# Where a matmul's operands lie in on-chip memory: activation tiles, weight halves and raw weights placed first, on multiples of 512 bytes

## The chip, the core and the metric

The kernel runs on one core of a Trainium2 chip. The metric is device time in microseconds, from the launch's first instruction to its last with what lies around them; three runs of the kernel before gave 998.23, 998.87 and 999.73 us, median 998.87. Beside it stands one profiled execution, whose span (first to last instruction) is 996.9 us.

## The reference

A trunk of two layers on 256 positions of width 1024, in float32. Each layer normalizes its input, makes one wide projection, runs four mixers side by side, merges them under gates and adds a gated feed-forward:

```python
h = rms_norm(x, norm1_g)
z = h @ w_in
za, zb, zc, zd, zg = jnp.split(z, IN_SPLITS, axis=-1)
ya = retention(za, ret_gn_g)
yb = conformer_conv(zb, conv_w, conv_b, conv_ln_g, conv_ln_b)
yc = spatial_gating(zc, gmlp_ln_g, gmlp_ln_b, gmlp_ws, gmlp_bs)
yd = swa_attention(zd, swa_q_g, swa_k_g, swa_sinks, rel_bias)
ys = jnp.stack([ya, yb, yc, yd], axis=2).astype(w_branch.dtype)
branches = jnp.einsum('bsnc,ncd->bsnd', ys, w_branch)
gates = jax.nn.sigmoid(zg.reshape(B, S, N_BRANCH, D_MODEL))
mix = jnp.sum(gates * branches, axis=2)
x = x + (mix @ w_out).astype(x.dtype)
h = rms_norm(x, norm2_g)
gt, up = jnp.split(h @ w_ffn_in, 2, axis=-1)
return x + ((jax.nn.silu(gt) * up) @ w_ffn_out).astype(x.dtype)
```

## The kernel before, in words

The 256 positions are two tiles of 128 (t = 0, 1). All large products have the activations as the stationary operand and the weights as the moving one. Float32 precision is reached with three matmuls of type float32r: each operand is split into a high part, which is the value rounded to that type, and a low part, which is the rest.

```python
nc.tensor.matmul(ps, xh, hs, start=start, stop=False)
nc.tensor.matmul(ps, xh, ls, start=False, stop=False)
nc.tensor.matmul(ps, xl, hs, start=False, stop=stop)
```

These are lines 137, 138 and 139, the method mm; nearly all of TensorE's work goes through them. The moving tile is wh, wl, wh in turn, the stationary tile the high part twice and the low part once. A stationary block is 128 x 128, that is 512 bytes in each partition; a moving block has 512 columns (2048 bytes in each partition) or, in the narrow pieces, 256.

The stationary tiles are of two kinds. hT (act_tile, L184; one buffer for each t) holds the normalized activations, and the merged mix before w_out; it has 8 blocks for the high part and 8 for the low. yT (y_tile, L187; four buffers) holds a mixer's output before its branch product, and a piece of the feed-forward's inner activation before w_ffn_out; it has 4 and 4 blocks. The method cols (L141) runs hT over a unit of weights; chunk (L593), gates (L731), project (L773) and the first half of ffn (L788) call it. The method branch (L749) and out_mm inside ffn (L823) run yT, by mm itself. In gates and in branch, twelve matmuls (4 blocks x 3) go to one bank of PSUM before the next bank is taken.

Weights come from memory in units of 1 MB, each of two halves of 512 KB (fetch, L97): a load into raw (six buffers), then in part (L112) ScalarE casts it into wh (L114) and VectorE writes the difference into wl (L115); wh and wl have eight buffers each. take (L123) keeps the loads two units ahead of use. The opening (L232) writes the first half's cast and difference by hand (L252, L254), and warms TensorE up with bf16 matmuls on a small tile, warm, which is both operands (L265).

Beside this, four mixers run as tasks that are advanced at ticks between chunks: softmax attention (L311 to L418), convolution, whose 31 taps are VectorE instructions (L443), retention, and the spatial gating, whose products have ws as the stationary and gv as the moving tile (L585). Transposes go through TensorE with the data as the stationary tile and the identity as the moving one (L164, L814). The reciprocal roots are powers on GpSimd (L181), with the constant tile nhalf as the exponent.

Every SBUF tile comes from a pool. Pools lie one behind the other in the order in which they are made, and the tiles of one pool in the order of their first use, each start rounded up to 32 bytes. So a small tile made early (nhalf, 40 bytes; derived, 20; col, 600; rel, 32) shifts the remainder of all behind it.

Of the kernel before, what the change touches and what calls it, by code (L numbers as in the profile page):

```python
# [8 lines left out]
F32 = mybir.dt.float32  # L9
BF16 = mybir.dt.bfloat16  # L10
F32R = mybir.dt.float32r
# [5 lines left out]
P = 128  # L17
# [11 lines left out]
BRANCHES = (3, 0, 2, 1)  # L29
FF_CHUNKS = (512, 512, 512, 512, 512, 256)  # L30
UNIT = 2048
C_QG, C_KG, C_CB, C_LG, C_LB, C_GB, C_SK, C_CW = 0, 1, 2, 6, 10, 14, 18, 26
NCOLS = C_CW + 4 * TAPS
K_COS, K_SIN, K_DEC, K_TRI = 0, 256, 512, 2048
# [45 lines left out]
class Kernel:  # L80
    def __init__(self, ctx, tc, a, out):
        self.tc, self.nc, self.a, self.out = tc, tc.nc, a, out
        pool = lambda name, **k: ctx.enter_context(tc.tile_pool(name=name, **k))
        self.cp = pool("cp", bufs=1)
        self.raw = pool("raw", bufs=6)
        self.hl = pool("hl", bufs=8)
        self.wk = pool("wk", bufs=10)
        self.b8 = pool("b8", bufs=2)
        self.sm = pool("sm", bufs=4)
        self.yp = pool("yp", bufs=4)  # L90
        self.acc = pool("acc", bufs=4, space=PSUM)
        self.mid = pool("mid", bufs=4, space=PSUM)
        self.dr = pool("dr", bufs=1, space=DRAM)
        self.units = {}
        self.next_load = 0

    def fetch(self, i, pin=False):  # L97
# [3 lines left out]
        for s in range(2):  # L101
            h = self.hl.tile([P, UNIT // 2], F32R, tag="h", name="wh")
            lo = self.hl.tile([P, UNIT // 2], F32R, tag="l", name="wl")
            src = self.raw.tile([P, UNIT // 2], F32, tag="raw", name="raw")
            dma = self.nc.sync.dma_start(out=src, in_=self.a["wu"][l, u, s])
# [75 lines left out]
        self.nc.gpsimd.tensor_tensor(out=out, in0=v, in1=self.nhalf[:, :n], op=ALU.pow)  # L181

    def act_tile(self, t):
        return self.cp.tile([P, 2, 8, P], F32R, tag=f"hT{t}", name=f"hT{t}")  # L184

    def y_tile(self):
        return self.yp.tile([P, 2, 4, P], F32R, tag="yT", name="yT")  # L187
# [35 lines left out]
    def setup(self):  # L223
        nc, cp, a = self.nc, self.cp, self.a
        self.x = [cp.tile([P, D], F32, name=f"x{t}") for t in range(T)]
        self.ident = cp.tile([P, P], F32, name="ident")
        self.nhalf = cp.tile([P, 10], F32, name="nhalf")
        nc.gpsimd.memset(self.nhalf, -0.5)
        self.uT = cp.tile([P, 4, TAPS - 1 + T * P], F32, name="uT")
        nc.gpsimd.memset(self.uT[:, :, : TAPS - 1], 0.0)  # L230
# [776 lines left out]
```

## Time and profile before

| | |
|---|---|
| median of three runs | 998.87 us |
| span of the profiled execution | 996.9 us |
| the median less the span, what lies around it | 2.0 us |
| TensorE busy | 971.7 us |
| VectorE busy | 684.1 us |
| ScalarE busy | 481.9 us |
| weight halves loaded | 320 of 512 KB |

The profile gives no time of its own for the profiled execution beside its span; the 2.0 us are taken as what lies around it. In the rows, PE is TensorE's matmuls, PEld its weight loads (of the stationary operand), DVE is VectorE, ACT ScalarE, POOL GpSimd, SP the engine that issues loads. A row of the timeline begins with the start and the duration in us; the duration of a matmul is a latency, and matmuls overlap, so the rate is read from start to start. A row of a group ends with its count, its busy time and mean duration (us, ns), and the idle time ahead of it with what ended it. A row of a stretch has, for each engine, busy time and number of instructions, then TensorE's granted clock, the DMA share and GB/s.

### The profile page before, as it was taken

The page shows a single profiled execution, that of the slowest core. Times are in us where ns is not written, and L with a number is a line of the kernel's source. Part 1 is how long each engine was busy: PE and PEld are TensorE (multiplying, and loading weights), DVE is VectorE, ACT ScalarE, POOL GpSimd, SP SyncE. Part 2 cuts the span into 40 slices and gives each one's busy share as a digit, 9 for nine tenths or more (in the row PEclk, how much of TensorE's full clock was granted, in tenths as well). Part 3 has the DMA queues.
Part 4 walks back from the last instruction along what each step waited for, and adds up shares of the span by engine and source line. Part 5 has one row for each costly group of instructions (what it writes and reads, how often), then busy time and mean ns, then how long its engine had stood idle before and what let it go on. Part 6 is the DMA issues. An engine that isn't in the chain of part 4 may idle for free.

```text
span 996.9 us, 12353 instructions
## 1 busy us (share of the span) xinstructions
PE 971.7 (97%) x4567; PEld 788.6 (79%) x4567; DVE 684.1 (69%) x1051; ACT 481.9 (48%) x688; POOL 39.1 (4%) x38
## 2 busy tenths in 40 slices
PE   7959999999999999999999999999999999999998
PEld 5837788888888888888988778888888888888887
DVE  6507999998767655546466699999865666555452
ACT  5308846444655444344355774644446455344440
POOL 1200002000000000000011000100000000000000
PEclk9989999999999999999999999999999999999999
DMA  9557565656554665655546246356555357655531
GB/s 354 159 84 280 189 212 174 214 184 194 186 167 153 212 209 170 195 183 174 188 167 210 88 166 204 124 180 191 189 176 192 100 186 237 198 178 180 189 97 43
DMA packets 51060, 178.89 MB, mean 179 GB/s; under 512 B 5520, under 2 KB 7992, under 8 KB 50872
## 3 DMA queue, kind: packets, MB, share of 16 engines
q1 hardware_dynamic: 50856, 178.04, 55.5%
q8 instruction: 36, 0.59, 0.2%
q14 instruction: 24, 0.20, 0.1%
q10 hardware_dynamic: 144, 0.07, 0.0%
HBM read 175.46 MB, written 2.62 MB: 179 GB/s over the span
## 4 chain that ended last, share of the span: by engine, by line
PE 91%; DMA 5%; DVE 2%; ACT 2%; issue 0%; SPq 0%; POOL 0%; DVEq 0%; ACTq 0%
PE acc L138 20%; PE acc L139 20%; PE acc L137 20%; PE mid L139 8%; PE mid L137 8%; PE mid L138 8%; DMA rd<-r 3%; PE mid L164 2%; PE mid L814 1%; DMA raw<-wu 1%; DVE wl L115 1%; ACT sc L386 1%; DMA bias<-rd 1%; PE mid L402 0%; DVE sc L372 0%
## 5 line engine op out<-in xcount | busy, mean ns | idle before, releaser
L115 DVE TENSOR_TENSOR wl<-raw,wh 128x1024 fp32r<-128x1024 f32 x319 | 385.6, 1223 | 193.4 <-ACT wh L114 190.8
L114 ACT CAST wh<-raw 128x1024 fp32r<-128x1024 f32 x319 | 331.8, 1052 | 328.1 <-PE acc L139 175.3
L137 PE MATMUL acc<-wh,hT 128*128 128x512 f32 (+1 forms) x640 | 253.5, 397 | 13.3 <-ACT wh L114 13.3
L138 PE MATMUL acc<-wl,hT 128*128 128x512 f32 (+1 forms) x640 | 251.7, 393 | 2.0 <-DVE wl L254 1.0
L139 PE MATMUL acc<-wh,hT 128*128 128x512 f32 (+1 forms) x640 | 251.3, 393 | 0.0
L137 PEld LDWEIGHTS acc<-wh,hT 128*128 128x128 f32 x640 | 120.9, 189 | 40.5 <-ACT wh L114 13.7
L137 PE MATMUL mid<-wh,hT 128*128 128x512 f32 (+1 forms) x384 | 145.8, 380 | 0.0
L138 PEld LDWEIGHTS acc<-wl,hT 128*128 128x128 f32 x640 | 121.1, 189 | 30.9 <-DVE wl L115 2.8
L139 PE MATMUL mid<-wh,hT 128*128 128x512 f32 (+1 forms) x384 | 144.8, 377 | 0.0
L138 PE MATMUL mid<-wl,hT 128*128 128x512 f32 (+1 forms) x384 | 144.7, 377 | 0.0
L139 PEld LDWEIGHTS acc<-wh,hT 128*128 128x128 f32 x640 | 120.8, 189 | 28.9 <-issue 0.6
L137 PE MATMUL acc<-wh,yT 128*128 128x512 f32 x304 | 119.1, 392 | 0.0
L138 PE MATMUL acc<-wl,yT 128*128 128x512 f32 x304 | 118.4, 389 | 0.0
L139 PE MATMUL acc<-wh,yT 128*128 128x512 f32 x304 | 118.1, 390 | 0.0
L443 DVE SCALAR_TENSOR_TENSOR ca<-uT,col,ca 128x256 f32<-128x256 f32 x240 | 101.9, 485 | 3.2 <-ACT ca L437 3.1
L139 PEld LDWEIGHTS mid<-wh,hT 128*128 128x128 f32 x384 | 72.3, 188 | 14.6
L138 PEld LDWEIGHTS mid<-wl,hT 128*128 128x128 f32 x384 | 72.4, 189 | 14.3
L137 PEld LDWEIGHTS mid<-wh,hT 128*128 128x128 f32 x384 | 72.3, 188 | 14.3
L139 PEld LDWEIGHTS acc<-wh,yT 128*128 128x128 f32 x304 | 57.0, 188 | 12.3 <-DVE yT L818 0.3
L137 PEld LDWEIGHTS acc<-wh,yT 128*128 128x128 f32 x304 | 57.1, 188 | 12.0 <-ACT yT L817 0.4
L138 PEld LDWEIGHTS acc<-wl,yT 128*128 128x128 f32 x304 | 57.1, 188 | 11.6
L737 ACT ACTIVATE gth<-acc 128x512 f32<-128x512 f32 x32 | 19.1, 597 | 32.8 <-PE acc L139 32.8
(141 smaller groups left out, 587.8 us busy)
## 6 DMA issues: line engine op xcount, KB each, us to landing
raw<-wu SPq DMA_DIRECT2D x320, 512.0 KB, 4.2
ng<-norms SPq DMA_DIRECT2D x4, 512.0 KB, 5.4
rows<-rows SPq DMA_DIRECT2D x2, 768.0 KB, 6.3
rd<-r SPq DMA_DIRECT2D x1, 1536.0 KB
const<-const SPq DMA_DIRECT2D x1, 1088.0 KB, 7.5
bias<-rd SPq DMA_DIRECT2D x1, 1024.0 KB, 5.7
out<-x SPq DMA_DIRECT2D x4, 256.0 KB, 2.0
x<-x SPq DMA_DIRECT2D x2, 256.0 KB, 3.4
```

Source lines behind the costliest of these rows:

```text
L114: nc.scalar.copy(h, src)
L115: nc.vector.tensor_tensor(out=lo, in0=src, in1=h.bitcast(F32), op=ALU.subtract)
L137: nc.tensor.matmul(ps, xh, hs, start=start, stop=False)
L138: nc.tensor.matmul(ps, xh, ls, start=False, stop=False)
L139: nc.tensor.matmul(ps, xl, hs, start=False, stop=stop)
L164: self.nc.tensor.transpose(ps[:, b * P : (b + 1) * P], src[:, b * P : (b + 1) * P], self.ident)
L386: nc.scalar.activation(sc[:, h, :], sc[:, h, :], AF.Exp, bias=nm[:, h : h + 1], accum_out=den[:, h : h + 1])
L443: nc.vector.scalar_tensor_tensor(out=self.ca[:, c, :], in0=self.uT[:, c, k : k + T * P], scalar=w[:, c, k : k + 1], in1=self.ca[:, c, :], ...
L737: self.nc.scalar.activation(th[t, n], ps[t], AF.Tanh, scale=0.5)
L814: nc.tensor.transpose(ps[:, b * P : (b + 1) * P], s[t][:, b * P : (b + 1) * P], self.ident)
```

## The change

Four pools (lead, ht, yp, hl) and raw are made first, the pool cp with the constants and x later; hT moves from cp to a pool of its own. The tile nhalf is widened from 10 to 96 columns and becomes the only one ahead of them: it starts at byte 16512, behind fixed constants, and its 384 bytes end at 16896, which is a multiple of 512. All tiles from there to the end of wk and b8 are multiples of 512 bytes long.

```diff
+LEAD = 96
...
-        self.cp = pool("cp", bufs=1)
+        self.lead = pool("lead", bufs=1)
+        self.ht = pool("ht", bufs=1)
+        self.yp = pool("yp", bufs=4)
+        self.hl = pool("hl", bufs=8)
         self.raw = pool("raw", bufs=6)
-        self.hl = pool("hl", bufs=8)
         self.wk = pool("wk", bufs=10)
         self.b8 = pool("b8", bufs=2)
+        self.cp = pool("cp", bufs=1)
         self.sm = pool("sm", bufs=4)
-        self.yp = pool("yp", bufs=4)
...
-        return self.cp.tile([P, 2, 8, P], F32R, tag=f"hT{t}", name=f"hT{t}")
+        return self.ht.tile([P, 2, 8, P], F32R, tag=f"hT{t}", name=f"hT{t}")
...
-        self.nhalf = cp.tile([P, 10], F32, name="nhalf")
+        self.nhalf = self.lead.tile([P, LEAD], F32, name="nhalf")
```

The start of each tile, as the built programs have it (byte in the partition, remainder by 512 and by 64):

| tile | before | by 512 | by 64 | after | by 512 | by 64 |
|---|---|---|---|---|---|---|
| hT of t = 0 | 33952 | 160 | 32 | 16896 | 0 | 0 |
| hT of t = 1 | 44192 | 160 | 32 | 25088 | 0 | 0 |
| yT, first of 4 | 212032 | 64 | 0 | 33280 | 0 | 0 |
| wh, first of 8 | 106816 | 320 | 0 | 49664 | 0 | 0 |
| wl, first of 8 | 139584 | 320 | 0 | 82432 | 0 | 0 |
| raw, first of 6 | 82240 | 320 | 0 | 115200 | 0 | 0 |
| wk (hn, fth, gv, ...) | 172352 | 320 | 0 | 139776 | 0 | 0 |
| ident | 24704 | 128 | 0 | 184832 | 0 | 0 |
| const | 53024 | 288 | 32 | 196704 | 96 | 32 |
| ws | 76096 | 320 | 0 | 219776 | 128 | 0 |

The number of instructions and their order stay the same on TensorE, ScalarE, GpSimd and in the load queue, but for the width of one memset. On VectorE one instruction moves, in the opening. These are VectorE's rows there before; x1 is the second tile's input, hT1 its activation tile, wl and wh the halves of weight units 2 and 3, and the number behind a name tells tiles of one name apart:

```order
L204 SCALAR_TENSOR_TENSOR hn_171<-x1_85,ms_169,ng_94 128x512
L115 TENSOR_TENSOR wl_179<-raw_180,wh_178 128x1024
L115 TENSOR_TENSOR wl_183<-raw_184,wh_182 128x1024
L173 TENSOR_TENSOR hT1_242<-mid_243,hT1_242 128x512
L115 TENSOR_TENSOR wl_191<-raw_192,wh_190 128x1024
L115 TENSOR_TENSOR wl_195<-raw_196,wh_194 128x1024
L173 TENSOR_TENSOR hT1_242<-mid_250,hT1_242 128x512
```

And these are the same rows after the change, where line numbers are larger by 3 and the numbers of names by 6:

```order
L207 SCALAR_TENSOR_TENSOR hn_177<-x1_91,ms_175,ng_100 128x512
L118 TENSOR_TENSOR wl_185<-raw_186,wh_184 128x1024
L118 TENSOR_TENSOR wl_189<-raw_190,wh_188 128x1024
L118 TENSOR_TENSOR wl_197<-raw_198,wh_196 128x1024
L176 TENSOR_TENSOR hT1_248<-mid_249,hT1_248 128x512
L118 TENSOR_TENSOR wl_201<-raw_202,wh_200 128x1024
L176 TENSOR_TENSOR hT1_248<-mid_256,hT1_248 128x512
```

The first half of hT1's low part (L173, then L176) has changed places with the difference of the first half of unit 3 that followed it.

## The prediction

> **What bounds the kernel now.** I read the page first: the busy times, the granted clock and the chain that ended last.
>
> ```profile
> span 996.9 us, 12353 instructions
> PE 971.7 (97%) x4567; PEld 788.6 (79%) x4567; DVE 684.1 (69%) x1051; ACT 481.9 (48%) x688; POOL 39.1 (4%) x38
> PEclk9989999999999999999999999999999999999999
> PE 91%; DMA 5%; DVE 2%; ACT 2%; issue 0%; SPq 0%; POOL 0%; DVEq 0%; ACTq 0%
> ```
>
> TensorE is busy for 97% of the span, it is 91% of the chain, and its clock is granted in full nearly throughout. So the end is set by how closely one matmul follows another. No matmul is removed; only a change of that spacing, or of a wait, can move the time. Next, the groups of instructions with their shapes kept apart, and from them the rows of line 137. Lines 138 and 139 issue one matmul each for every one of line 137, so each count stands three times.
>
> ```profile
> L137 PE MATMUL acc<-wh,hT 128*128 128x512 f32 x608 | 244.4, 403 | 13.3 <-ACT wh L114 13.3
> L137 PE MATMUL mid<-wh,hT 128*128 128x512 f32 x320 | 127.6, 399 | 0.0
> L137 PE MATMUL acc<-wh,yT 128*128 128x512 f32 x304 | 119.1, 392 | 0.0
> L137 PE MATMUL acc<-wh,hT 128*128 128x256 f32 x32 | 9.1, 285 | 0.0
> L137 PE MATMUL mid<-wh,hT 128*128 128x256 f32 x64 | 18.1, 283 | 0.0
> ```
>
> That is 3 x (608 + 320) = 2784 matmuls of 512 columns with hT as the stationary operand, 3 x 304 = 912 with yT, and 3 x (32 + 64) = 288 of 256 columns with hT. The means (403 and 399 against 392 ns) are latencies that overlap, and they already differ between hT and yT. What counts is the distance from start to start, which I took from the timeline of TensorE, at a place where a branch (L756, stationary yT) is followed by the gates of the next (L146, stationary hT), and those by another branch. Both loops send twelve matmuls into one bank, with moving tiles from the same buffers.
>
> ```profile
> 216.58 0.40 PE L137 MATMUL acc<-wh,yT 128*128 128x512 f32 x1
> 227.24 0.39 PE L139 MATMUL acc<-wh,yT 128*128 128x512 f32 x1
> 227.47 0.39 PE L137 MATMUL acc<-wh,hT 128*128 128x512 f32 x1
> 249.72 0.39 PE L139 MATMUL acc<-wh,hT 128*128 128x512 f32 x1
> 249.96 0.40 PE L137 MATMUL acc<-wh,yT 128*128 128x512 f32 x1
> ```
>
> The branch's 48 matmuls (4 banks x 4 steps x 3) take 227.47 - 216.58 = 10.89 us, 226.9 ns each; the gates' 96 (4 banks x 8 steps x 3) take 249.96 - 227.47 = 22.49 us, 234.3 ns each. Same shape, type, clock and buffers of the moving side, and 7.4 ns between them. What differs is the stationary tile's place: hT starts 160 bytes past a multiple of 512 (32 past one of 64), yT 64 bytes past (0 past one of 64). That is the argument of this prediction: the spacing depends on where the operands lie.
>
> **The change part by part.** *hT's matmuls, 512 columns.* After the change hT lies like yT on a multiple of 64, and relative to the moving tile both cases are alike in their low 8 bits (yT now: 64 against 320, which differ by 256; then: 0 against 0). So I take yT's spacing, 226.9 ns, for all: 7.4 ns less for each of 2784. How far can it go? The least that 512 columns take in this trace is the three bf16 matmuls of the warm-up:
>
> ```profile
> 10.34 0.81 PE L265 MATMUL mid<-warm 128*128 128x512 bf16 x3
> L265 PE MATMUL mid<-warm x17: 379/379/634, 1.2 to 10.8; 128*128 128x512 bf16 x17
> ```
>
> (810 - 379) / 2 = 215.5 ns. So the bounds are 215.5 ns below, and above nothing in the chip's rows excludes more than today's 234.3. The Trainium skill (TensorE: Matmul & The Clock Gate, section Back-to-back issue gap) gives a warm matmul's gap as its columns over 2.4 GHz plus 2.5 ns, an estimate of 215.8 ns from that page; the trace agrees for the warm-up's 215.5 and not for these fp32r matmuls at 226.9 and 234.3, and by the rule for all of them the time would be that of the second rival below.
>
> Not every nanosecond of this shortens the run. Three stretches end with something other than TensorE:
>
> ```profile
> 40.02 33.44 DMA rd<-r
> 564.78 3.94 ACT sc L386 x16
> 0.00:20.00 20.00, 7.13 (x27) 4.81 (x28) 1.38 (x2) 1.79 (x3) 1.00 0.91 339
> 40.00:80.00 40.00, 24.83 (x97) 18.59 (x96) 0.00 (x0) 0.00 (x0) 0.83 0.55 110
> 80.00:106.00 26.00, 18.07 (x65) 11.43 (x63) 0.00 (x0) 0.00 (x0) 1.00 0.53 196
> 553.00:583.00 30.00, 19.81 (x77) 14.14 (x76) 0.00 (x0) 0.00 (x0) 1.00 0.23 76
> ```
>
> The first two rows are from the chain in order of time, the others are the stretches of the instructions on hT (after length: TensorE, its weight loads, VectorE, ScalarE). The opening waits for loads and weight parts, 40 to 80 us for the bias table's round trip through memory, 80 to 106 and 553 to 583 us for the softmax tasks on ScalarE and VectorE. I write off all 27 + 97 + 65 + 77 = 266 matmuls there. Gain: (2784 - 266) x 7.4 ns = 18.6 us.
>
> *hT's matmuls, 256 columns.* No row shows them with a well-placed stationary tile.
>
> ```profile
> 29.84 0.28 PE L139 MATMUL acc<-wh,hT 128*128 128x256 f32 x1
> 31.02 0.39 PE L137 MATMUL acc<-wh,hT 128*128 128x512 f32 x1
> 350.23 1.03 PE L814 MATMUL mid<-ident,fth 128*128 128x128 f32 x8
> L814 PE MATMUL mid<-ident,fth 128*128 128x128 f32 x88 | 11.5, 272 | 0.0
> ```
>
> Ten of them take 1.18 us, 118 ns each. Bounds: no gain, and the (1030 - 272) / 7 = 108 ns at which transposes, each with its own weight load, follow each other: 288 x 10 ns = 2.9 us. I take the same share as at 512 columns, 118 x 7.4 / 234.3 = 3.7 ns: 288 x 3.7 ns = 1.1 us.
>
> *yT's matmuls.* They move from 64 to 0 past a multiple of 512, and their moving tiles from 320 to 0. Between a gain of 11.4 ns (to 215.5) and a loss I take nothing, as they are nearest to their own row.
>
> *VectorE's cover.* Where the convolution's taps run, VectorE is nearly full:
>
> ```profile
> 106.00:225.00 119.00, 118.58 (x548) 97.32 (x549) 116.55 (x207) 63.76 (x82) 9.01 (x5) 1.00 0.63 205
> 583.00:700.00 117.00, 117.00 (x541) 95.89 (x541) 113.45 (x212) 58.30 (x76) 4.40 (x4) 1.00 0.57 182
> ACT wh L114 <- PE acc L139: 175.3, 119, 5.3
>   PE acc L138: 1.9, 3
> ```
>
> It has 2.45 and 3.55 us free; a TensorE faster by 3% would shorten either stretch by up to 3.7 us. ScalarE's splitting waits 175.3 us for TensorE to give up weight buffers and TensorE itself waited 1.9 us in all for VectorE's wl (last row, who waited for wl), so weight parts are ahead and cover a lag. I charge 0.5 us, between 0 and 1.3.
>
> *Other engines' operands* move too. VectorE takes as long where it reads the constants from 32 past a multiple of 64 as where all lies on 64, and ScalarE writes hT as fast as yT:
>
> ```profile
> L507 DVE TENSOR_TENSOR r<-acc,const 128x512 f32<-128x512 f32 x8 | 5.5, 687 | 6.6 <-PE acc L139 6.6
> L515 DVE TENSOR_TENSOR r<-r,r 128x512 f32<-128x512 f32 x8 | 5.5, 688 | 0.1
> L171 ACT ACTIVATE hT<-mid 128x512 fp32r<-128x512 f32 x24 | 13.3, 595 | 15.0 <-PE mid L164 14.8
> L817 ACT ACTIVATE yT<-mid 128x512 fp32r<-128x512 f32 x20 | 10.8, 593 | 0.0
> ```
>
> So nothing there. The longer memset of nhalf costs a tenth of a microsecond on GpSimd, far ahead of its first reader. The loads of raw are the same bytes in the same order, to other addresses; I take nothing for them.
>
> *The moved VectorE instruction.* In the opening one subtraction (L115) now stands ahead of the first half of the second hT.
>
> ```profile
> 18.47 2.36 DVE L115 TENSOR_TENSOR wl<-raw,wh 128x1024 fp32r<-128x1024 f32 x2
> 20.74 0.69 DVE L173 TENSOR_TENSOR hT<-mid,hT 128x512 fp32r<-128x512 f32 x1
> 19.38 1.05 ACT L114 CAST wh<-raw 128x1024 fp32r<-128x1024 f32 x1
> 23.02 0.39 PE L139 MATMUL acc<-wh,hT 128*128 128x512 f32 x1
> ```
>
> The subtraction's wh is there at 20.43, so it runs from 20.83 to about 22.0 and hT's low half is written at about 22.7; its first reader, L139, starts at 23.02. Queued behind it are the next subtraction and the second half, which is needed twelve matmuls later. Cost 0, at most 0.5 us if TensorE comes earlier.
>
> **Sum.** 18.6 + 1.1 - 0.5 = 19.2 us off the profiled execution: a span of 977.7 us. The median of the three runs, 998.87, stands 2.0 us above the span, so I forecast 979.7 us.
>
> **The rivals.** *Slower: equal remainders collide.* After the change the stationary and the moving tile of every large matmul start at the same byte modulo 512; today they are 160 (hT) or 256 (yT) apart. If the two reads then meet in the same part of the memory, the spacing rises for all. One group shows equal remainders today, the gating's ws and gv, both 320 past a multiple of 512.
>
> ```profile
> 163.66 1.95 PE L585 MATMUL mid<-gv,ws 128*128 128x128 f32 x16
> L585 PE MATMUL mid<-gv,ws 128*128 128x128 f32 x32 | 3.9, 275 | 0.0
> ```
>
> They follow each other by (1950 - 275) / 15 = 111.7 ns, 3.1% over the transposes' 108.3, whose operands are 192 bytes apart. With 3.1% on today's spacings, 7.3 and 7.0 ns, the price is 2784 x 7.3 + 912 x 7.0 ns = 20.3 + 6.4 = 26.7 us, time 1025.6. It decides from a common spacing of (2784 x 234.3 + 912 x 226.9) / 3696 = 232.5 ns on. Against it: transposes are another kind of instruction, so the 3.1% need not be a collision, and the warm-up's operands start at the same byte (one tile is both) and run at 215.5. One in ten.
>
> *More than forecast: all fall to the floor.* If the 11.4 ns that yT has over 215.5 are also a matter of place: (2784 - 266) x 18.8 = 47.3, 912 x 11.4 = 10.4 and 2.9 us, 60.6 in all. But VectorE would then bound the two stretches above, which TensorE would leave about 9 us each sooner and VectorE 2.45 and 3.55: some 12 us back. Time 998.9 - 60.6 + 12 = 950; half way to the floor, about 965. For it speaks that yT is not on 128 today either; against it, that yT's spacing holds so steadily. 15 in a hundred for all of it, 5 for something between it and the forecast.
>
> *No change: place does not set the spacing.* Then the 7.4 ns come from something that goes with hT and not with its remainder, such as the distance of its region from the weights', and the time stays at 998.9. The Trainium skill (SBUF — State Buffer, section Who interferes with whom) gives TensorE one read port for the moving operand and another, independent, for weight loads, and says it never waits on anyone; its box on cachelines names lines of 16 bytes, which every tile here starts on already. By that rule the sum would be 0; the trace speaks against it as far as two equal loops run 7.4 ns apart. One in ten.
>
> **How the numbers follow.** Forecast 60%, to the floor 15%, between 5%, no change 10%, collision 10%. A measurement of this kernel tells about 0.2%, 2 us, from no change. Faster 0.80, same 0.10, slower 0.10. The forecast's own range is 974 to 985 (7.4 ns give or take a third at hT, 256 columns and VectorE at their bounds). Leaving out the collision and the lower part of the floor case, the range is 955 to 999.
>
> **What would show it.** In the changed kernel's timeline the distance of hT's starts should be 227 ns as yT's are, in every stage, with the same counts of groups; TensorE's mean for hT at 512 columns should fall from about 399 to about 390. VectorE should be 98% busy or more from 106 to 222 us, with TensorE's waits for wl or acc no longer than 1 us. If hT stays at 234, place is not the cause; if yT moves as well, 64 bytes were not the grain; if the spacing falls and the time does not, VectorE took over.

## The result, and the profile after

| | median | lowest to highest | runs |
|---|---|---|---|
| before, on the same chip | 999.3 us | 998.23 to 1000.21 | 4 |
| after | 981.62 us | 981.12 to 982.4 | 4 |

The ratio is 0.9822, 95% interval 0.9808 to 0.9836: faster by 1.8%. The forecast was 979.7 us. The profiled execution took 982.4 us, 0.8 above the median of its kind; its span is 980.3 us, 16.6 less than before, where the sum had 19.2.

The page of the changed kernel, the same rows as were read of the kernel before:

```profile
span 980.3 us, 12353 instructions
PE 956.2 (98%) x4567; PEld 789.3 (81%) x4567; DVE 681.7 (70%) x1051; ACT 482.5 (49%) x688; POOL 38.7 (4%) x38
PEclk9988999999999999999999999999999999999999
PE 90%; DMA 4%; ACT 3%; DVE 2%; issue 1%; SPq 0%; POOL 0%; ACTq 0%; DVEq 0%
```

The same instructions, the clock granted as before, and TensorE still 90% of the chain. Its busy time alone fell, by 15.5 us; the other engines' stayed within 2.4 us. So neither VectorE nor a transfer has become the bound. The groups with shapes apart (line numbers are larger by 3) show which matmuls it came from:

```profile
L140 PE MATMUL acc<-wh,hT 128*128 128x512 f32 x608 | 241.3, 397 | 13.7 <-ACT wh L117 13.7
L140 PE MATMUL mid<-wh,hT 128*128 128x512 f32 x320 | 125.4, 392 | 0.0
L140 PE MATMUL acc<-wh,yT 128*128 128x512 f32 x304 | 119.1, 392 | 0.0
L140 PE MATMUL acc<-wh,hT 128*128 128x256 f32 x32 | 9.2, 288 | 0.0
L140 PE MATMUL mid<-wh,hT 128*128 128x256 f32 x64 | 18.3, 285 | 0.0
```

Counts are equal. For hT with 512 columns the mean latency fell from 403 and 399 to 397 and 392 ns; for yT it stayed at 392; with 256 columns it rose, from 285 and 283 to 288 and 285. The rate shows at the place that was read before, a branch on yT, the gates on hT and the next branch:

```profile
214.32 0.39 PE L140 MATMUL acc<-wh,yT 128*128 128x512 f32 x1
224.97 0.39 PE L142 MATMUL acc<-wh,yT 128*128 128x512 f32 x1
225.20 0.39 PE L140 MATMUL acc<-wh,hT 128*128 128x512 f32 x1
246.73 0.39 PE L142 MATMUL acc<-wh,hT 128*128 128x512 f32 x1
246.96 0.39 PE L140 MATMUL acc<-wh,yT 128*128 128x512 f32 x1
```

yT's 48 take 225.20 - 214.32 = 10.88 us, 226.7 ns each; hT's 96 take 246.96 - 225.20 = 21.76 us, 226.7 ns each, where they took 234.3. The two loops now run alike. Over the whole trace, I took the distance of every two neighbouring starts of one kind (leaving out pauses), some 2640, 878 and 275 pairs. These means are the measure of all that follows:

| spacing, ns | hT, 512 columns | yT, 512 columns | hT, 256 columns |
|---|---|---|---|
| before | 234.2 | 227.2 | 118.0 |
| after | 227.1 | 227.0 | 119.7 |

VectorE's two full stretches, as stretches of the trace (VectorE is the third pair after the length, TensorE the first):

```profile
106.00:222.00 116.00, 115.39 (x545) 96.52 (x545) 115.28 (x206) 64.15 (x83) 8.58 (x5) 1.00 0.64 209
583.00:690.00 107.00, 107.00 (x510) 89.86 (x509) 105.45 (x200) 54.55 (x70) 4.39 (x4) 1.00 0.56 183
  PEld acc L141: 3.5, 5
  PE acc L141: 0.9, 2
```

It is 99.4 and 98.6% busy, and TensorE still hardly stops: 0.61 us without a matmul in the first stretch, none in the second. The last two rows are who waited for wl in the whole run: weight loads 3.5 us, matmuls 0.9 us.

### The profile page after: what moved, and what is told of

It is laid out like the page before. It is cut to its first block, busy times and chain, and to the rows that moved or that the text cites. A ratio compares the mean times of both kernels' runs of the same rounds, so it can differ in the third digit from the quotient of the medians.

```text
span 980.3 us, 12353 instructions
## 1 busy us (share of the span) xinstructions
PE 956.2 (98%) x4567; PEld 789.3 (81%) x4567; DVE 681.7 (70%) x1051; ACT 482.5 (49%) x688; POOL 38.7 (4%) x38
## 4 chain that ended last, share of the span: by engine, by line
PE 90%; DMA 4%; ACT 3%; DVE 2%; issue 1%; SPq 0%; POOL 0%; ACTq 0%; DVEq 0%
PE acc L141 20%; PE acc L142 20%; PE acc L140 20%; PE mid L140 8%; PE mid L142 8%; PE mid L141 8%; DMA raw<-wu 3%; PE mid L167 2%; ACT sc L389 1%; PE mid L817 1%; ACT sc L395 1%; DVE wl L118 1%; DMA ng<-norms 1%; ACT wh L117 0%; PE mid L588 0%
## 5 line engine op out<-in xcount | busy, mean ns | idle before, releaser
L140 PE MATMUL acc<-wh,hT 128*128 128x512 f32 (+1 forms) x640 | 250.5, 392 | 13.7 <-ACT wh L117 13.7
L141 PE MATMUL acc<-wl,hT 128*128 128x512 f32 (+1 forms) x640 | 248.0, 387 | 1.0 <-DVE wl L118 0.9
L142 PE MATMUL acc<-wh,hT 128*128 128x512 f32 (+1 forms) x640 | 247.9, 387 | 0.0
L140 PE MATMUL mid<-wh,hT 128*128 128x512 f32 (+1 forms) x384 | 143.7, 374 | 0.0
L142 PE MATMUL mid<-wh,hT 128*128 128x512 f32 (+1 forms) x384 | 142.7, 372 | 0.0
L141 PE MATMUL mid<-wl,hT 128*128 128x512 f32 (+1 forms) x384 | 142.6, 371 | 0.0
L141 PE MATMUL acc<-wl,yT 128*128 128x512 f32 x304 | 118.4, 389 | 0.0
L740 ACT ACTIVATE gth<-acc 128x512 f32<-128x512 f32 x32 | 19.2, 599 | 30.9 <-PE acc L142 30.9
```

Source lines behind the costliest of these rows:

```text
L740: self.nc.scalar.activation(th[t, n], ps[t], AF.Tanh, scale=0.5)
```

## The experiments

The theory on record was that a stationary tile has to start on a multiple of 64 bytes. The other explanation is that what counts is the distance between the two operands. I write D for the start of the moving tile less the start of the stationary one, modulo 256 bytes. Blocks follow each other by multiples of 512 bytes, so one D holds for all of a tile. Before, hT had (320 - 160) = 160 and yT (320 - 64) = 256, that is 0; after, both have 0. The kernel before was timed anew beside each group of runs (medians 999.84, 999.66 and 999.72 us).

**hT alone to a multiple of 64.** In the kernel before, 32 bytes ahead of hT shift it from 160 to 192 past a multiple of 512 (the constants behind it in its pool move with it), and a pad restores raw and all behind it. D for hT becomes 128.

```diff
+        pad2 = pool("pad2", bufs=1)
+        pad2.tile([P, 120], F32, name="pad2")
         self.raw = pool("raw", bufs=6)
...
+        cp.tile([P, 8], F32, name="pad")
```

> The kernel before, with hT alone moved by 32 bytes (from 160 to 192 past a multiple of 512, so onto a multiple of 64); wh, wl, raw and yT keep their remainders. Own theory (the stationary tile has to start on a multiple of 64): hT's starts 226.7 ns apart as yT's, all of the gain, about 981.5 us. Rival 1 (it takes the multiple of 512, or wh and wl must move too): hT stays at 234.3, 999 us. Rival 2 (the region of memory decides, not the remainder): 234.3, 999 us.

Measured: 995.02 us, ratio 0.9947 (0.9932 to 0.9962). hT's spacing is 232.4 ns, not 227. That is a quarter of the way to yT's spacing. The theory on record fell with this run.

**hT off by 32, everything off by 32, the moving tiles off by 32.** Three variants of the changed kernel. The first puts hT alone 32 past a multiple of 512 (D 224), the second shifts all tiles by 32 (D 0 again, on no multiple of 64), the third shifts wh and wl alone (D 32 for hT and for yT).

```diff
 # first (with a pad behind ht), and second (without it)
-LEAD = 96
+LEAD = 104
...
 # first
+        pad_ht = pool("pad_ht", bufs=1)
+        pad_ht.tile([P, 120], F32, name="pad_ht")
...
 # third: 32 bytes ahead of hl, and a pad behind it
+        pad_yp = pool("pad_yp", bufs=1)
+        pad_yp.tile([P, 8], F32, name="pad_yp")
...
+        pad_hl = pool("pad_hl", bufs=1)
+        pad_hl.tile([P, 120], F32, name="pad_hl")
```

> The changed kernel, with hT alone moved to 32 past a multiple of 512; all else on multiples of 512 as it was. Own theory (the stationary tile's multiple of 64): hT back at about 234.3 ns, yT at 226.7, about 998 to 999 us. Rival (region): hT stays at 226.7, 981.6 us.

> The changed kernel, with the lead tile 32 bytes longer, so that hT, yT, wh, wl and raw all start 32 past a multiple of 512. If each operand's own place by 64 counts: hT and yT both at about 234.3 ns, 982 + 2784 x 7.6 + 912 x 7.6 ns less the hidden part, about 1008 us. If the distance between the two operands counts (now 0 as in the changed kernel): 226.7 for both, 981.6 us.

> The changed kernel, with wh and wl alone moved to 32 past a multiple of 512; hT and yT stay on multiples of 512. If only the stationary tile's own place counts: 226.7 ns for both, 981.6 us. If the moving tile's counts as well, or the distance between the two: hT and yT at about 234 ns, about 1008 us.

| | us | ratio to before | hT | yT | hT, 256 columns |
|---|---|---|---|---|---|
| hT off by 32 | 995.91 | 0.9954 (0.9939 to 0.9969) | 233.3 | 227.0 | 118.4 |
| all off by 32 | 983.49 | 0.9832 (0.9817 to 0.9847) | 227.1 | 227.0 | 119.8 |
| moving tiles off by 32 | 1001.4 | 1.0015 (1.0005 to 1.0025) | 233.3 | 233.3 | 117.0 |

The same place of the timeline in each: first hT off by 32, where the gates on hT begin and where the next branch begins.

```profile
224.95 0.39 PE L142 MATMUL acc<-wh,hT 128*128 128x512 f32 x1
247.34 0.39 PE L142 MATMUL acc<-wh,yT 128*128 128x512 f32 x1
```

Then all off by 32:

```profile
226.35 0.39 PE L140 MATMUL acc<-wh,hT 128*128 128x512 f32 x1
248.11 0.39 PE L140 MATMUL acc<-wh,yT 128*128 128x512 f32 x1
```

And the moving tiles off by 32, with the start of the branch on yT ahead:

```profile
215.03 0.39 PE L144 MATMUL acc<-wh,yT 128*128 128x512 f32 x1
226.22 0.39 PE L144 MATMUL acc<-wh,hT 128*128 128x512 f32 x1
248.62 0.39 PE L144 MATMUL acc<-wh,yT 128*128 128x512 f32 x1
```

96 matmuls on hT take 22.39, 21.76 and 22.40 us. hT lies 32 past a multiple of 512 in the first two and is slow in one, fast in the other; in the third hT and yT lie on multiples of 512 and both are slow (yT's 48 take 11.19 us, 233.1 ns). So it is not the stationary tile's own place, and not the moving tile's, but the distance between them. The third variant is the one in this study that is slower than the kernel before: yT, which was well placed by chance, loses its 6 ns as well. The kernel with everything off by 32 has a median 1.9 us above the changed kernel's. In the profiled executions, whose spans are 1.0 us apart, the difference lies early: the first matmul behind the softmax starts at 107.96 us against 106.81, and from there to the end of the span the two take 873.3 and 873.5 us.

**More distances.** In one run, hT at D 64 with yT at D 96; in another, hT at D 192. Both shift pools by pads as above.

> The changed kernel with two more distances between the moving and the stationary tile's start, modulo 256: 64 for hT, 96 for yT (wh and wl on multiples of 512 as before). Theory (the distance modulo 256 sets the spacing, and 0 alone lets the starts settle): hT and yT both between 231 and 235 ns on average, about 1003 us in all. Rival (any multiple of 64 between them is good): hT 226.7, yT 233 to 234, about 988 us. Side question: a distance under 226.7 ns, towards 215.5, would show that the rest of the spacing is a matter of place too.

> The changed kernel with hT at a distance of 192 modulo 256 from wh and wl; yT stays at 0. Theory (distance modulo 256, 0 alone settles): hT 231 to 235 ns, yT 226.7, about 995 to 997 us. Rival (multiples of 64 are good): both at 226.7, 981.6 us.

Then hT at D 16, 240 and 8, by a wider tile of which hT is a part, so that all other large tiles keep their remainders (D 16 was run once, and timed later as the same kernel):

```diff
-        return self.ht.tile([P, 2, 8, P], F32R, tag=f"hT{t}", name=f"hT{t}")
+        wide = self.ht.tile([P, 2112], F32R, tag=f"hT{t}", name=f"hT{t}")
+        return wide[:, 60:2108].rearrange("p (s k m) -> p s k m", s=2, k=8)
```

with 4:2052 for D 240 and 62:2110 for D 8.

> The changed kernel with hT taken 16 bytes ahead of a multiple of 256 inside a wider tile, so 16 away from wh and wl; yT stays at 0. Theory (only a distance of 0 settles): hT 230 to 235 ns, 992 to 998 us. Rival (what counts is coarser than 16 bytes): 226.7, 981.6 us. Under 226.7 would be a placement better than the change's.

> The changed kernel with hT 16 bytes past a multiple of 256, so at a distance of 240 modulo 256 (16 on the other side of 0); yT at 0. If the spacing depends on how near the distance is to 0, whichever side: 227 to 228 ns, about 982 us. If it rises from 0 upwards and wraps (240 next to 224, which gave 233.3): 230 to 233 ns, 989 to 995 us.

> The changed kernel with hT 8 bytes ahead of a multiple of 256, a distance of 8. Theory (within 16 bytes of 0 the spacing is that of 0): 226.5 to 228 ns, 981 to 983 us. Rival (a multiple of 16 is needed, whatever the distance): 232 ns or more, 993 us or more.

> The kernel of the run with a distance of 16, timed: 227.7 ns at 512 columns and 118 at 256 against 227.1 and 119.7 of the change work out to 2518 x 0.6 - 288 x 1.6 ns = 1.0 us over the change: 981 to 983.5 us, no version that beats it.

All distances in one table; the kernel's time stands where hT alone has that D and yT has 0.

| D of hT | spacing of hT, ns | us | ratio to before |
|---|---|---|---|
| 0 (the change) | 227.1 | 981.62 | 0.9822 (0.9808 to 0.9836) |
| 8 | 233.3 | 995.52 | 0.9959 (0.9944 to 0.9974) |
| 16 | 227.7 | 983.01; the single run 981.87 | 0.9832 (0.9817 to 0.9847) |
| 32 | 233.3 | 1001.4, yT at 32 too | 1.0015 (1.0005 to 1.0025) |
| 64 | 229.0 | 992.04, one run, yT at 96: 233.4 ns | |
| 128 | 232.4 | 995.02 | 0.9947 (0.9932 to 0.9962) |
| 160 (before) | 234.2 | 999.3 | 1 |
| 192 | 233.4 | 997.03, one run | |
| 224 | 233.3 | 995.91 | 0.9954 (0.9939 to 0.9969) |
| 240 | 230.2 | 989.75 | 0.9897 (0.988 to 0.9913) |

There is no slope that one could follow: 8 bytes off costs as much as 32, and 16 bytes off costs half a nanosecond. Three expectations missed: for D 64 I had 231 to 235 ns, or 226.7 if any multiple of 64 were good, and it came between; for D 16 I had 230 to 235; for D 8 I had the good spacing. None of the distances is better than D 0. The mean at D 240 is of two kinds of stretch within one run. These are the gates (96 matmuls between the rows), which follow a branch on yT:

```profile
226.42 0.39 PE L140 MATMUL acc<-wh,hT 128*128 128x512 f32 x1
248.18 0.39 PE L140 MATMUL acc<-wh,yT 128*128 128x512 f32 x1
```

and this is part of a run that began behind transposes at 325.26, in the same kernel:

```profile
330.24 0.39 PE L140 MATMUL mid<-wh,hT 128*128 128x512 f32 x1
347.04 0.39 PE L140 MATMUL mid<-wh,hT 128*128 128x512 f32 x1
```

The first goes at 21.76 / 96 = 226.7 ns. The second has 72 matmuls in 16.80 us, 233.3 ns, and keeps it to its end. So there are two paces that a series can lock into. hT has 30 series of 36 matmuls or more; at D 240 the four behind a branch and nine others go at 226.7 ns and 17 at 233.3, so the way in which a series begins seems to decide. At D 16 series lock into 226.7 or 228.3 ns. At D 0 all 30 reach 226.7: those behind a branch from their first step, most others after a first step of some 314 ns and at most nine uneven ones (224 to 236 ns). At D 8, 32, 128, 160, 192 and 224 none gets there.

**Only the low half of hT off by 32.** hT's high half stays at D 0, its low half, which only the third matmul of each step uses, goes to D 224.

```diff
+class Halves:
+    def __init__(self, wide, gap):
+        self.part = [wide[:, o : o + 1024].rearrange("p (k m) -> p k m", k=8) for o in (0, 1024 + gap)]
...
-        return self.ht.tile([P, 2, 8, P], F32R, tag=f"hT{t}", name=f"hT{t}")
+        wide = self.ht.tile([P, 2112], F32R, tag=f"hT{t}", name=f"hT{t}")
+        return Halves(wide, 8)
```

> The changed kernel with hT's low half alone moved by 32 bytes, so that of three matmuls on a block the first two (L137, L138 of the kernel before) have the distance 0 and the third (L139) has 224 modulo 256. If the reads that meet are those of a matmul's moving tile and of the weight load for the next: only the matmul ahead of the low half is off, a third of the loss, about 229 ns on average, 987 us. If the distance must hold throughout for the starts to settle: nearly all of the loss, 231 to 233 ns, 992 to 995 us.

Measured in one run: 995.03 us, hT's mean spacing 233.2 ns, yT's 227.0. One misplaced load in three costs nearly as much as three, as expected for a distance that must hold throughout; a loss at one matmul in three alone would have given about 229 ns. Where it costs is seen in the timeline, where L149, L150 and L151 are the three matmuls of a step:

```profile
229.93 0.40 PE L149 MATMUL acc<-wh,hT 128*128 128x512 f32 x1
230.16 0.40 PE L150 MATMUL acc<-wl,hT 128*128 128x512 f32 x1
230.40 0.39 PE L151 MATMUL acc<-wh,hT 128*128 128x512 f32 x1
230.63 0.40 PE L149 MATMUL acc<-wh,hT 128*128 128x512 f32 x1
```

From start to start, over some 850 to 900 pairs each, it is 232.3 ns after L149, 238.3 after L150 and 228.6 after L151. With all of hT at D 224 the three are alike, 233.2 to 233.4 ns. The longest is the one in which L150 runs and the weight load for L151, the misplaced one, goes on beside it. That points to the moving read of one matmul meeting the weight load of the next, and not to a matmul's two operands of its own.

**Series with narrower weight loads.** At the end of the changed kernel, five series of 16 matmuls on a tile of their own: 128, 64 and 32 stationary columns at D 0, then 128 and 32 at D 224. They lengthen the kernel by some 15 us, so the kernel's time (996.55) says nothing.

```diff
+        for first, cols in ((0, 128), (0, 64), (0, 32), (8, 128), (8, 32)):
+            ps = self.bank()
+            for _ in range(16):
+                nc.tensor.matmul(ps[:cols, :], pr[:, first : first + cols], pr[:, 512:1024], start=True, stop=True)
```

> The changed kernel with five series of 16 float32r matmuls of 512 columns on one tile behind its end: stationary blocks of 128, 64 and 32 columns at distance 0, then 128 and 32 columns at distance 224. It measures the spacing by itself; its total time says nothing. If the time over 215.5 ns is the meeting of the moving read with the next weight load: 226.7 at 128 columns, less with 64 and 32 columns (about 221 and 218), and about 233 at 128 and under 220 at 32 columns for distance 224. If it is float32r's own rate: 226.7 whatever the width at distance 0.

Stretches of the timeline, each within one series, in their order:

```profile
975.20 3.56 PE L931 MATMUL mid<-pr 128*128 128x512 f32 x15
979.06 3.15 PE L931 MATMUL mid<-pr 128*64 128x512 f32 x13
982.74 3.17 PE L931 MATMUL mid<-pr 128*32 128x512 f32 x13
986.44 3.43 PE L931 MATMUL mid<-pr 128*128 128x512 f32 x14
991.10 2.08 PE L931 MATMUL mid<-pr 128*32 128x512 f32 x8
```

Less one latency of 0.39 to 0.40 us, and divided by the steps between: 227, 230, 232, 233 and 240 ns. The last row is the settled part of its series, whose first steps were shorter; over all 15 steps it has 237 ns. First, the effect is there on a bare series without any other work of the kernel: 227 against 233 for 128 columns. Second, a load of fewer columns does not shorten the spacing, although it takes less time itself (108 ns of 32 columns against 188 of 128):

```profile
L931 PEld LDWEIGHTS mid<-pr 128*128 128x128 f32 x32 | 6.0, 188 | 1.4
L931 PEld LDWEIGHTS mid<-pr 128*32 128x32 f32 x32 | 3.5, 108 | 3.9
```

It makes it longer, at D 0 and at D 224. So the price is not in proportion to what is loaded, and 226.7 ns is not a lower floor plus the time of a collision that shrinks with the load. Neither expectation for fewer columns was met: less spacing if the two reads meet, or 226.7 for every width at D 0. (These matmuls also write fewer output partitions, `ps[:cols, :]`, so more than the load differs.) The Trainium skill (TensorE: Matmul & The Clock Gate, section Back-to-back issue gap) gives 512 columns a gap of some 216 ns alone and 131 ns in a sustained stream of loads and matmuls; no series of fp32r with 512 columns here settled below 226.7, with 32 columns loaded or with 128.

## Why the prediction was right, and where its reason was not

*The bound, the direction and the main term* held. The spacing of hT's 512 columns was to fall by 7.4 ns for 2518 matmuls, 18.6 us. It fell by 234.2 - 227.1 = 7.1 ns: 17.9 us. The settled pace is a little below what was forecast (226.7 against 226.9), but most series that begin behind transposes or a pause have up to nine uneven steps first, which the one clean place in the profile could not show. The mean latency of hT's matmuls fell from 399 to 393 ns, where about 390 was expected.

*256 columns* had the wrong sign. I took the same share as at 512, 3.7 ns less; they went from 118.0 to 119.7, 1.8 ns more. Over the 264 that start after 25 us this is 0.5 us lost in place of 1.1 gained: 1.6 of the 2.6 us that the span lacks. At D 32, where 512 columns are at 233.3, 256 columns are at their best, 117.0. The two widths want different distances, and no row of the trace before could tell.

*VectorE's cover*, 0.5 us, was not needed: the stretches are 99.4 and 98.6% full and TensorE stops 0.61 us in the first, where before it stopped 119.00 - 118.58 = 0.42 us in 119. Matmuls waited 0.9 us for wl, within the 1 us expected; weight loads waited 3.5 us, 4.2 before.

*The hidden stretches* gave nothing back up to 106 us, as written off. The chain of the kernel before and that of the changed one, at the first matmuls after the softmax, then the same matmul with hT off by 32 and with everything off by 32:

```profile
106.42 0.51 PE acc L138
```

```profile
106.81 0.50 PE acc L141
```

```profile
104.25 0.50 PE L143 MATMUL acc<-wl,hT 128*128 128x512 f32 x1 [0.60 <-DVE wl L120]
107.96 0.50 PE L141 MATMUL acc<-wl,hT 128*128 128x512 f32 x1 [0.61 <-DVE wl L118]
```

The changed kernel is 0.4 us behind there, and all its 16.6 us come after. The 0.4 us say nothing of placement: in the runs this start lies anywhere from 104.25 to 107.96 us, and it is earliest with hT off by 32, where hT is slow. With that, 17.9 - 0.5 - 0.4 = 17.0; the last 0.4 us I can't place, and the spans of four runs of the changed kernel alone go from 979.0 to 980.3 us.

*The moved VectorE instruction* and *other engines' operands* cost nothing that shows: TensorE's 151st matmul starts at 35.94 us before and 35.92 after, and no engine's busy time rose by more than 0.7 us. The first half of hT1's low part is written at 22.75 us (22.7 in the forecast), ahead of its first reader:

```profile
22.06 0.69 DVE L176 TENSOR_TENSOR hT<-mid,hT 128x512 fp32r<-128x512 f32 x1
23.26 0.39 PE L142 MATMUL acc<-wh,hT 128*128 128x512 f32 x1
```

Nor is the gain due to the new order: the variants with hT and with the moving tiles off by 32 have it too, and their hT has 233.3 ns.

*yT unmoved* held, to 0.2 ns, although its first buffer went from byte 212032 to 33280. So the region does not matter, which rules out the one cause that the rival of no change named; hT off by 32 lies in the new region, 32 bytes from the changed kernel's place, and is slow.

*The reason* failed, at this step: "So I take yT's spacing, 226.9 ns, for all", with the stationary tile's place (32 or 0 past a multiple of 64) as the cause. The sentence before had the right fact in its second half, that relative to the moving tile both cases are alike in their low 8 bits, and the forecast rested on it by luck: the number would have been the same for either reason. hT alone on a multiple of 64 was worth 4.8 us, not 18; all tiles off that multiple at the same distance kept the gain.

*The range* of 974 to 985 us holds the result, but is narrower than the bounds given for its terms: with hT's gain a third off, 256 columns between 0 and 2.9 us and VectorE between 0 and 1.3, the sum lies between 11.1 and 27.7 us, the time between 971 and 988.

*The rivals.* Equal remainders do not collide at 512 columns; they are the best of the cases tried. The gating's row, on which that rival rested, kept its 1.95 us although D of gv and ws went from 0 to 128:

```profile
162.63 1.95 PE L588 MATMUL mid<-gv,ws 128*128 128x128 f32 x16
```

The floor of 215.5 ns is not reached, by any placement tried. That TensorE's two reads don't touch each other, the rule of the Trainium skill (SBUF — State Buffer, section Who interferes with whom) behind the rival of no change, doesn't agree with the runs: moving either operand by 32 bytes, without any other change of the matmuls, takes 6 ns more for each.

*What stays open* is the mechanism. Shown are the dependence on the distance, and that a series locks into one of a few paces. That the moving read meets the next weight load fits the three matmuls of a step above, but it is argued. Why 8 and 32 bytes off are bad and 16 is not, why 256 columns differ, and why narrower loads are slower is not explained by it; a period of the moving stream against the load would have to be measured with other column counts, which wasn't tried.

## What to carry to other kernels

When TensorE is the bound, read start-to-start spacings by stationary tile, not latencies: two loops of the same shape that differ by a few per cent can differ in nothing but where their operands lie. For fp32r with 512 moving columns, give the moving and the stationary tile the same start modulo 256 bytes, by the order and the lengths of the pools; a small tile made early can undo it for all behind it. Test a rule of placement by moving both operands together, then each alone, before believing that one tile's alignment is the cause.

## What the runs showed of the hardware

- fp32r matmuls of 512 columns with a load of 128 each follow each other by 226.7 ns once settled at D 0, and by 233 to 234 in the mean at six of the ten other distances tried (8, 32, 96, 160, 192, 224); the whole kernel is 1.8% apart by it, with the same instructions.
- Transposes and the gating's products, 128 columns in f32 without fp32r, showed nothing of it at the two distances that each had: the gating's 16 took 1.95 us at D 0 and at D 128, and transposes of fth followed each other by 109 ns at D 64 and at D 0.
- There are locked paces. Before, hT's spacings repeat every seven matmuls (232, 237, 238, 231, 234, 235, 233 ns, 234.3 in the mean); at D 0 they are even (226, 227, 227 in whole ns); at D 240 series settle at 226.7 or 233.3.
- 256 columns lie between 117.0 ns (D 32) and 119.9 (D 128), in another order of distances than 512 columns.
- Loading 32 columns instead of 128 made the spacing longer, 232 against 227 ns at D 0 and 240 against 233 at D 224.
